# Huber loss, 8192 x 8192: another split of the element-wise work between VectorE and ScalarE, half-tile pieces, and a tail whose pieces are ordered by hand

## The chip, the cores and the metric

The kernel runs on one core of one Trainium2 chip. The metric is device time in microseconds for one execution of the whole kernel, the median of several executions. "Tile" below means one slab of 128 partitions by up to 10432 fp32 columns.

## The reference

```python
def reference(pred, target):            # both 8192 x 8192 fp32
    delta = 1.0
    diff = pred - target
    abs_diff = np.abs(diff)
    return np.where(abs_diff <= delta, 0.5 * diff**2, delta * (abs_diff - 0.5 * delta))
```

With d = pred - target the result is d*d/2 where |d| is at most 1, and |d| - 1/2 elsewhere. It is element-wise: every element of the two inputs is read once and every element of the result is written once, 268 MB each.

## The kernel before, in words

The three arrays are taken as flat, and cut into 51 tiles: 50 of 128 x 10432 elements (5216 KB each) and a last one, number 50, of 128 x 2688. A tile of prediction lives in one of three buffers `a` (`NA = 3`), a tile of target in one of two buffers `b` (`NB = 2`). The result is computed in place in `a` and stored from there.

*Transfers.* All loads and stores are issued by SyncE, in the order of the list `order` that `plan` builds. In the middle of the kernel one turn is: store tile i, load target of tile i+2, load prediction of tile i+3. SyncE takes them strictly in order: a transfer that must wait holds up all behind it. A store waits for the tile's last VectorE instruction; a target load waits until its buffer is free, that is until tile i has been computed; a prediction load waits until the store of tile i has landed, because it goes into the same buffer. In the page and the timeline the stores carry line L136 and the loads L145. For the last tiles `order` is written out one by one: `z` is the number of the last tile (50), and tiles 48 and 49 have their target loaded in two parts, columns 0 to 7040 (`h0`) and 7040 to 10432 (`h1`), so that the first part can be put ahead of other transfers.

*Compute.* Each tile is cut into three pieces of 3520, 3520 and 3392 columns (tile 50 into two of 1344). A piece goes through `first` and later through `second`:

- `first`: VectorE subtracts target from prediction into `a` (L97) and clamps the difference to [-1, 1] into `b` (L98). ScalarE then makes `a` absolute (L101), subtracts 1 and cuts off at 0 (Relu, L103), and squares `b` (L104).
- `second`: VectorE adds half of `b` to `a` (L113). This is the result, since min(|d|,1)^2 / 2 + max(|d|-1, 0) is the Huber loss. For the last piece of a tile (the set `vec`) VectorE also does the work of L103, as L110.

The list `comp` holds these steps in the order in which they are issued to the engines. VectorE and ScalarE each execute in that order. For most tiles it is first, first, second, first, second, second; for the last three tiles (`LAST`) the closing step of a tile is put behind the opening step of the next.

`compute_until` issues steps from `comp` until the tile, or the part of it, that the next transfer needs is finished. The engines' order is written out by hand in this way; the waits between engines are placed by the framework from what each instruction reads and writes, and from the release of buffers.

Of the kernel before, what the change touches and what calls it, by code (L numbers as in the profile page):

```python
# [1 line left out]

# [4 lines left out]

P = 128
W = 10432
NA, NB = 3, 2  # L10
LAST = 3


def plan(total):

    tiles = [(c, min(W, total - c)) for c in range(0, total, W)]
    n = len(tiles)
    wid = [w for _, w in tiles]

    def cut(i, k):
        step = -(-wid[i] // (k * 64)) * 64
        edge = list(range(0, wid[i], step)) + [wid[i]]
        return list(zip(edge, edge[1:]))

    whole = lambda kind, i: [(kind, i, 0, wid[i])]  # L30
    order = []
    for lo, hi in cut(0, 2):
        order += [("b", 0, lo, hi), ("a", 0, lo, hi)]
    order += whole("a", 1) + whole("b", 1) + whole("a", 2)

    z = n - 1
    for i in range(z - 6):
        order += whole("s", i) + whole("b", i + 2) + whole("a", i + 3)

    split = cut(z - 1, 3)[1][1]  # L40
    h0, h1 = (0, split), (split, W)
    order += whole("s", z - 6) + whole("b", z - 4) + whole("a", z - 3)
    order += whole("b", z - 3) + whole("s", z - 5)
    order += [("b", z - 2, *h0)] + whole("a", z - 2)
    order += whole("s", z - 4) + [("b", z - 2, *h1)]
    order += [("b", z - 1, *h0)] + whole("a", z - 1)
    order += whole("s", z - 3) + [("b", z - 1, *h1)]
    order += whole("b", z) + whole("a", z) + whole("s", z - 2)
    order += [("s", z - 1, lo, hi) for lo, hi in cut(z - 1, 3)]
    order += [("s", z, lo, hi) for lo, hi in cut(z, 2)]  # L50
    pieces = [(i, lo, hi) for i in range(n) for lo, hi in cut(i, 3 if wid[i] > W // 2 else 2)]
    comp = []
    late = []
    for p in pieces:
        comp.append(("first",) + p)
        late.append(p)
        i, lo, hi = p
        if i < n - LAST and hi == wid[i]:
            comp += [("second",) + q for q in late]
            late = []  # L60
        elif len(late) > 1:
            comp.append(("second",) + late.pop(0))
    comp += [("second",) + q for q in late]
    vec = {p for p in pieces if p[2] == wid[p[0]]}
    return tiles, order, comp, vec


@with_exitstack
def kernel(
    ctx: ExitStack,  # L70
    tc: tile.TileContext,
    pred: bass.AP,
    target: bass.AP,
    out: bass.AP,
):
    nc = tc.nc
    f32 = mybir.dt.float32
    Alu = mybir.AluOpType
    Act = mybir.ActivationFunctionType
    Eng = mybir.EngineType  # L80

    flat = {k: x.rearrange("r c -> (r c)") for k, x in zip("bas", (target, pred, out))}
    tiles, order, comp, vec = plan(flat["a"].shape[0] // P)

    const = ctx.enter_context(tc.tile_pool(name="const", bufs=1))
    pool_a = ctx.enter_context(tc.tile_pool(name="pool_a", bufs=NA))
    pool_b = ctx.enter_context(tc.tile_pool(name="pool_b", bufs=NB))

    neg1 = const.tile([P, 1], f32)
    nc.vector.memset(neg1, -1.0)  # L90

    A, B = {}, {}

    def first(i, lo, hi):

        a, b = A[i][:, lo:hi], B[i][:, lo:hi]
        nc.vector.tensor_tensor(out=a, in0=a, in1=b, op=Alu.subtract)  # L97
        nc.vector.tensor_scalar(  # L98
            out=b, in0=a, scalar1=-1.0, scalar2=1.0, op0=Alu.max, op1=Alu.min
        )  # L100
        nc.scalar.activation(out=a, in_=a, func=Act.Abs)  # L101
        if (i, lo, hi) not in vec:
            nc.scalar.activation(out=a, in_=a, func=Act.Relu, bias=neg1)  # L103
        nc.scalar.activation(out=b, in_=b, func=Act.Square)  # L104

    def second(i, lo, hi):

        a, b = A[i][:, lo:hi], B[i][:, lo:hi]
        if (i, lo, hi) in vec:
            nc.vector.tensor_scalar(  # L110
                out=a, in0=a, scalar1=-1.0, scalar2=0.0, op0=Alu.add, op1=Alu.max
            )
        nc.vector.scalar_tensor_tensor(  # L113
            out=a, in0=b, scalar=0.5, in1=a, op0=Alu.mult, op1=Alu.add
        )

    ready = {i: 0 for i in range(-max(NA, NB), len(tiles))}
    for i in range(-max(NA, NB), 0):
        ready[i] = W

    def compute_until(i, hi):
        while ready[i] < hi:
            what, j, l, h = comp.pop(0)
            if what == "first":
                first(j, l, h)
            else:
                second(j, l, h)
                ready[j] = h

    with tc.manual_schedule(engines={Eng.SP, Eng.DVE, Eng.Activation}):  # L130
        for kind, i, lo, hi in order:
            at, w = tiles[i]
            dram = flat[kind][P * at : P * (at + w)].rearrange("(p m) -> p m", p=P)
            if kind == "s":
                compute_until(i, hi)
                nc.sync.dma_start(out=dram[:, lo:hi], in_=A[i][:, lo:hi])  # L136
                continue
            have, pool, name, bufs = (
                (A, pool_a, "a", NA) if kind == "a" else (B, pool_b, "b", NB)
            )  # L140
            if i not in have:
                if i >= bufs:
                    compute_until(i - bufs, tiles[i - bufs][1])
                have[i] = pool.tile([P, W], f32, name=name)
            nc.sync.dma_start(out=have[i][:, lo:hi], in_=dram[:, lo:hi])  # L145


# [1 line left out]
_INS = ['pred', 'target']  # L149
_OUTS = [((8192, 8192), 'float32')]  # L150


# [23 lines left out]
```

## Time and profile before

| | |
|---|---|
| median of 9 runs | 1874.13 us (1874.03 to 1875.05) |
| the profiled execution's own time | 1875.05 us |
| span of that execution | 1873.3 us |
| VectorE busy | 1517.4 us, 81% |
| ScalarE busy | 1238.9 us, 66% |
| DMA | 805.41 MB, mean 430 GB/s |
| VectorE L97, 128 x 3520 | 3822 ns |
| VectorE L98, 128 x 3520 | 1994 ns |
| VectorE L113, 128 x 3520 | 3825 ns |
| ScalarE L101 / L103 / L104, 128 x 3520 | 3129 / 3229 / 3120 ns |
| SyncE waiting for stores to land, before a load | 1193.8 us in 48 waits |
| SyncE waiting for VectorE's L113, before a store | 467.9 us in 50 waits |

The span runs from the program's first instruction on any engine to its last; the own time of an execution is a little longer. In lines of the profile's timeline the first number is the start in microseconds from the span's start, the second the duration, then engine, source line, operation and what it writes and reads; a bracket at the end gives the idle time of the engine before the instruction and what ended it. `SPq` marks SyncE's issue of a transfer: the duration there is that of the issue, not of the transfer. DMA work is shown as a share of the 16 DMA engines' time and in GB/s.

### The profile page before, as it was taken

Reading aid. Unit: us, or ns where it says so; the run is one execution under the profiler, and the core shown is the slowest. Engines: PE = TensorE matmul, PEld = TensorE weight load, DVE = VectorE, ACT = ScalarE, POOL = GpSimd, SP = SyncE. Lnnn points to the kernel's source line nnn. Section 1 sums busy time; section 2 is a strip of 40 time slices with the busy share of each in tenths; the row PEclk is TensorE's granted clock in tenths of the full one; section 3 lists DMA queues with packets and bytes.
Section 4 is the critical chain, followed back from the end, with each engine's and each line's share of the span. In section 5 each row is a group of like instructions: output and inputs, shape, how many; then the busy total and the mean of one; then the engine's idle time right before and its main releaser. Section 6 shows DMA issues by size and latency. Waiting matters only on the chain.

```text
span 1873.3 us, 1374 instructions
## 1 busy us (share of the span) xinstructions
DVE 1517.4 (81%) x508; ACT 1238.9 (66%) x406; POOL 0.2 (0%) x4
## 2 busy tenths in 40 slices
DVE  5887878787788778887878787888778887878898
ACT  4567756765776577657756775676577657756776
POOL 0000000000000000000000000000000000000000
DMA  9999999999999999999999999999999999999999
GB/s 413 428 434 434 431 437 429 433 435 431 437 430 432 435 431 437 430 435 434 430 437 430 433 436 429 437 431 432 437 429 436 432 432 437 429 435 433 387 427 383
DMA packets 23051, 805.41 MB, mean 430 GB/s; under 512 B 2560, under 2 KB 2560, under 8 KB 2816
## 3 DMA queue, kind: packets, MB, share of 16 engines
q1 hardware_dynamic: 23040, 805.32, 99.8%
q14 instruction: 11, 0.09, 0.0%
HBM read 536.87 MB, written 268.44 MB: 430 GB/s over the span
## 4 chain that ended last, share of the span: by engine, by line
DMA 53%; DVE 25%; ACT 17%; issue 4%; SPq 1%; ACTq 0%; DVEq 0%
DMA b<-in_target_dram 46%; DVE a L97 10%; DVE a L113 10%; ACT b L104 8%; DVE b L98 5%; ACT a L101 4%; ACT a L103 4%; DMA out_dram<-a 4%; DMA a<-in_pred_dram 3%; SPq L136 0%; DVE a L110 0%; SPq L145 0%; ACTq L171 0%; DVEq L97 0%; DVEq L113 0%
## 5 line engine op out<-in xcount | busy, mean ns | idle before, releaser
L101 ACT ACTIVATE a<-a 128x3520 f32<-128x3520 f32 (+1 forms) x152 | 467.0, 3072 | 605.2 <-DVE b L98 598.4
L113 DVE SCALAR_TENSOR_TENSOR a<-b,a 128x3520 f32<-128x3520 f32 (+1 forms) x152 | 570.3, 3752 | 200.3 <-ACT b L104 200.1
L97 DVE TENSOR_TENSOR a<-a,b 128x3520 f32<-128x3520 f32 (+1 forms) x152 | 569.5, 3747 | 141.5 <-DMA b<-in_target_dram 119.4
L104 ACT ACTIVATE b<-b 128x3520 f32<-128x3520 f32 (+1 forms) x152 | 465.3, 3061 | 0.0
L103 ACT ACTIVATE a<-a,neg 128x3520 f32<-128x3520 f32 (+1 forms) x101 | 324.3, 3211 | 3.3
L98 DVE TENSOR_SCALAR b<-a 128x3520 f32<-128x3520 f32 (+1 forms) x152 | 297.4, 1957 | 5.2
L110 DVE TENSOR_SCALAR a<-a 128x3392 f32<-128x3392 f32 (+1 forms) x51 | 96.9, 1899 | 0.0
L101 ACT ACT_TABLE_LOAD x1 | 1.3, 1283 | 16.3 <-DMA a<-in_pred_dram 16.3
L90 DVE MEMSET neg<- 128x1 f32 x1 | 0.1, 59 | 0.8 <-PEq L160 0.8
L160 POOL MEMSET const-bfloat16-1.0<- 128x1 bf16 x1 | 0.1, 103 | 0.0
L160 POOL MEMSET const-uint8-127<- 128x1 uint8 x1 | 0.1, 103 | 0.0
L160 POOL MEMSET const-float32-1.0<- 128x1 f32 x1 | 0.1, 100 | 0.0
L160 POOL MEMSET const-float32-0.0<- 128x1 f32 x1 | 0.1, 99 | 0.2 <-issue 0.2
## 6 DMA issues: line engine op xcount, KB each, us to landing
a<-in_pred_dram SPq DMA_DIRECT2D x49, 5216.0 KB, 24.6
out_dram<-a SPq DMA_DIRECT2D x49, 5216.0 KB, 27.1
b<-in_target_dram SPq DMA_DIRECT2D x47, 5216.0 KB, 39.0
b<-in_target_dram SPq DMA_DIRECT2D x2, 3520.0 KB, 13.6
out_dram<-a SPq DMA_DIRECT2D x2, 1760.0 KB, 17.2
b<-in_target_dram SPq DMA_DIRECT2D x2, 1696.0 KB, 39.1
b<-in_target_dram SPq DMA_DIRECT2D x1, 2624.0 KB, 8.9
a<-in_pred_dram SPq DMA_DIRECT2D x1, 2624.0 KB, 15.1
```

What stands on the lines that cost most here:

```text
L90: nc.vector.memset(neg1, -1.0)
L97: nc.vector.tensor_tensor(out=a, in0=a, in1=b, op=Alu.subtract)
L98: nc.vector.tensor_scalar(out=b, in0=a, scalar1=-1.0, scalar2=1.0, op0=Alu.max, op1=Alu.min)
L101: nc.scalar.activation(out=a, in_=a, func=Act.Abs)
L103: nc.scalar.activation(out=a, in_=a, func=Act.Relu, bias=neg1)
L104: nc.scalar.activation(out=b, in_=b, func=Act.Square)
L110: nc.vector.tensor_scalar(out=a, in0=a, scalar1=-1.0, scalar2=0.0, op0=Alu.add, op1=Alu.max)
L113: nc.vector.scalar_tensor_tensor(out=a, in0=b, scalar=0.5, in1=a, op0=Alu.mult, op1=Alu.add)
L160: nc = _bacc.Bacc("TRN2", target_bir_lowering=False, num_devices=1)
```

## The change

Tiles 0 to 45 are computed in two pieces, of 5248 and 5184 columns, by three steps, each done for both pieces before the next:

- `d`: VectorE subtracts; ScalarE makes the difference absolute, in `a`.
- `t`: VectorE forms t = min(|d|, 1) * |d| in place; ScalarE copies t/2 into `b`.
- `h`: VectorE takes max(t - 1/2, t/2), the result. (For |d| at most 1, t = d*d and t/2 is the larger; beyond it, t = |d| and t - 1/2 is the larger.)

The last five tiles keep the former method (`f` and `g`; with capital letters VectorE does L103's work in place of ScalarE). Their order is written out piece by piece in `TAIL`: the letter is the step, the first number counts tiles back from the last, the second is the piece. `F4.0` is the opening step of piece 0 of tile 46, `g3.2` the closing step of piece 2 of tile 47.

Tiles 46 to 49 have their target loaded in two parts (before: 48 and 49), and the order of the transfers near the end is changed: the second part of tile 48's target stands ahead of the store of tile 46, and tile 49's first target part behind that store, as before. `compute_until` now goes by columns that are closed, since pieces of a tile no longer close in order.

```diff
-LAST = 3
+TAIL = """
+F4.0 f4.1 G4.0 f4.2 g4.1 f3.2 F3.1 g4.2 F3.0 G3.1 G3.0 F2.0 F2.1 f2.2 G2.1 g3.2 G2.0 g2.2
+F1.0 f1.1 G1.0 f1.2 f0.0 g1.1 f0.1 g1.2 g0.0 g0.1
+"""
...
-    split = cut(z - 1, 3)[1][1]
-    h0, h1 = (0, split), (split, W)
-    order += whole("s", z - 6) + whole("b", z - 4) + whole("a", z - 3)
-    order += whole("b", z - 3) + whole("s", z - 5)
-    order += [("b", z - 2, *h0)] + whole("a", z - 2)
-    order += whole("s", z - 4) + [("b", z - 2, *h1)]
-    order += [("b", z - 1, *h0)] + whole("a", z - 1)
+    third = cut(z - 1, 3)
+    h0, h1 = (0, third[1][1]), third[2]
+    order += whole("s", z - 6) + [("b", z - 4, *h0), ("b", z - 4, *h1)]
+    order += whole("a", z - 3) + [("b", z - 3, *h0), ("b", z - 3, *h1)]
+    order += whole("s", z - 5)
+    order += [("b", z - 2, *h0)] + whole("a", z - 2) + [("b", z - 2, *h1)]
+    order += whole("s", z - 4) + [("b", z - 1, *h0)] + whole("a", z - 1)
     order += whole("s", z - 3) + [("b", z - 1, *h1)]
     order += whole("b", z) + whole("a", z) + whole("s", z - 2)
-    order += [("s", z - 1, lo, hi) for lo, hi in cut(z - 1, 3)]
+    order += [("s", z - 1, lo, hi) for lo, hi in third]
     order += [("s", z, lo, hi) for lo, hi in cut(z, 2)]
...
+    comp = [(op, i, lo, hi) for i in range(z - 4) for op in "dth" for lo, hi in cut(i, 2)]
+    for word in TAIL.split():
+        back, piece = word[1:].split(".")
+        i = z - int(back)
+        comp.append((word[0], i, *cut(i, 3 if i < z else 2)[int(piece)]))
+    return tiles, order, comp
...
+        if op == "d":
+            sub(a, b)
+            act(out=a, in_=a, func=Act.Abs)
+        elif op == "t":
+            vec.scalar_tensor_tensor(
+                out=a, in0=a, scalar=1.0, in1=a, op0=Alu.min, op1=Alu.mult
+            )
+            act(out=b, in_=a, func=Act.Copy, scale=0.5)
+        elif op == "h":
+            vec.scalar_tensor_tensor(
+                out=a, in0=a, scalar=-0.5, in1=b, op0=Alu.add, op1=Alu.max
+            )
+        elif op in "fF":
+            sub(a, b)
+            vec.tensor_scalar(
+                out=b, in0=a, scalar1=-1.0, scalar2=1.0, op0=Alu.max, op1=Alu.min
+            )
+            act(out=a, in_=a, func=Act.Abs)
+            if op == "f":
+                act(out=a, in_=a, func=Act.Relu, bias=neg1)
+            act(out=b, in_=b, func=Act.Square)
+        else:
+            if op == "G":
+                vec.tensor_scalar(
+                    out=a, in0=a, scalar1=-1.0, scalar2=0.0, op0=Alu.add, op1=Alu.max
+                )
+            vec.scalar_tensor_tensor(
+                out=a, in0=b, scalar=0.5, in1=a, op0=Alu.mult, op1=Alu.add
+            )
+        if op in "hgG":
+            left[i] -= hi - lo
+            closed.update((i, c) for c in range(lo, hi, 64))
...
-                compute_until(i, hi)
+                compute_until(lambda: all((i, c) in closed for c in range(lo, hi, 64)))
...
-                    compute_until(i - bufs, tiles[i - bufs][1])
+                    compute_until(lambda: left[i - bufs] == 0)
```

## The prediction

> **What bounds the kernel now.** I read the page's totals first, then its slices.
>
> ```profile
> span 1873.3 us, 1374 instructions
> DVE 1517.4 (81%) x508; ACT 1238.9 (66%) x406; POOL 0.2 (0%) x4
> ...
> DMA  9999999999999999999999999999999999999999
> GB/s 413 428 434 434 431 437 429 433 435 431 437 430 432 435 431 437 430 435 434 430 437 430 433 436 429 437 431 432 437 429 436 432 432 437 429 435 433 387 427 383
> ```
>
> VectorE is at 81%, but the DMA engines are busy in every slice at about 433 GB/s. A full tile transfer (128 x 10432 fp32, 5.34 MB) therefore takes 5.34/0.433 = 12.34 us, and a tile's three transfers 37.0 us. Only the first slice and the last three are short. Next the timeline of a middle tile, DMA issues and VectorE's first operation:
>
> ```profile
> 942.00 0.34 SPq L136 DMA_DIRECT2D out_dram<-a  x1
> 942.43 0.38 SPq L145 DMA_DIRECT2D b<-in_target_dram  x1
> 944.56 3.83 DVE L97 TENSOR_TENSOR a<-a,b 128x3520 f32<-128x3520 f32 x1 [2.59 <-DMA b<-in_target_dram]
> ...
> 969.12 0.33 SPq L145 DMA_DIRECT2D a<-in_pred_dram  x1
> ...
> 979.03 0.34 SPq L136 DMA_DIRECT2D out_dram<-a  x1
> ```
>
> The period is 979.03 - 942.00 = 37.03 us: DMA's 37.0. VectorE waits 2.59 us per tile for target. The store issued at 979.03 queues behind a prediction load that runs to about 969.1 + 24.6 (the page's median to landing) = 993.7, so compute has some 14.7 us of slack there. Last the end of the kernel, as windows (start:end, length, busy of DVE, ACT and POOL, clock, DMA share, GB/s) and timeline:
>
> ```profile
> 1750.00:1752.00 2.00, 2.00 (x2) 2.00 (x2) 0.00 (x0) 1.00 1.01 438
> 1752.00:1754.00 2.00, 1.57 (x2) 1.45 (x1) 0.00 (x0) 1.00 0.68 292
> 1754.00:1756.00 2.00, 2.00 (x1) 0.00 (x0) 0.00 (x0) 1.00 0.24 104
> 1756.00:1758.00 2.00, 2.00 (x2) 0.00 (x0) 0.00 (x0) 1.00 0.12 46
> 1758.00:1760.00 2.00, 2.00 (x1) 0.00 (x0) 0.00 (x0) 1.00 0.99 296
> ```
> ```profile
> 1753.49 3.69 DVE L113 SCALAR_TENSOR_TENSOR a<-b,a 128x3392 f32<-128x3392 f32 x1 [0.43 <-ACT b L104]
> ...
> 1757.21 0.33 SPq L145 DMA_DIRECT2D b<-in_target_dram  x1
> 1760.43 0.33 SPq L145 DMA_DIRECT2D a<-in_pred_dram  x1
> ```
>
> The queue runs dry once: about 0.3 + 0.76 + 0.88 of each 2 us, some 3.8 us of an average engine. The load that ends it, tile 48's first target part, goes out at 1757.21, just after tile 46's *last* VectorE operation ends (1753.49 + 3.69 = 1757.18), though it overwrites only columns 0 to 7040, which were finished at 1751.2. A target buffer is released as a whole tile. And at least one DMA engine was not dry: 0.12 of 16 engines is two still storing tile 45, whose landing let the 1760.43 issue go. That last engine lags the rest by some 5 us (they stop about 1754, it about 1760), loses nothing in the gap, and sets the end.
>
> **The Trainium skill.** "DMA: Bandwidth & Descriptors", section "Anatomy of one DMA — SWDGE (gpsimd) path", says that DMA engines do not wait on semaphores; the issuing sequencer does, and they eat their queues. The trace agrees: each late SP issue shows as missing GB/s. Its section "Why a DMA increments its semaphore by 16 and not by 1" says that the engines finish independently and only the full count means landed: the drain from share 0.68 to 0.12 shows that skew. "VectorE: DVE Perf Modes", section "The TRN2 errata — SBUF-src ops pay a fixed extra latency per instruction", gives (N+151)/0.96 ns for fp32 tensor_tensor; at 3520 that is 3824 ns, the trace has 3822, and SCALAR_TENSOR_TENSOR 3825.
>
> **The change, part by part.**
> *Steady tiles 0 to 45.* Per tile it removes three subtracts, three clamps, three combines and one Relu on VectorE (33 us busy) and adds two each of subtract, the new t and the new max step, on 5248 and 5184 columns. No row has those widths; from the subtract's groups by shape, 1344 (1552) and 3520 (3822), the slope is 1.043 ns, so 5.62 and 5.56 us. t reads one tile on both inputs, which no row does; at best 2.9 us (twice as fast, like a clamp), at worst 11 us (each element fetched twice); I take 5.62, as for L113's two inputs. Back-to-back operations overlap 0.08 us, so a tile is 3 x (5.62 + 5.56) - 0.4 = 33.1 us. ScalarE's half-tile Abs or Copy, scaled from 3129 and 3029 ns, takes about 4.6 us, less than the VectorE half behind which it hides. 33.1 is below 37.03, and below today's first-operation-to-store 34.5, so stores go out about 1 us earlier into a backlog of 14.7: worth 0. Without the DMA cover it would be 46 x 37 again only if t passed 7.5 us.
> *First tile.* Compute starts when its second half lands (28.6), and ends near 56.3 against 53.5; the loads queued run to about 65: 0.
> *Split target loads.* Tiles 46 and 47 give two more DMA instructions, 0.4 us of SP each behind a backlog: 0, 0.8 uncovered.
> *The hand-ordered tail* is what counts. In the built program the load of tile 48's first target part still waits for VectorE's last piece of tile 46 (g4.2), and tile 49's for the last piece of tile 47 (g3.2). Both were moved later.
>
> First gap. g4.2 now stands behind f3.2 and F3.1, which need tile 47's second target part. Target 46 landed just before 1722.74; prediction 47 and target 47 follow, 2 x 12.34, so 1747.4. Then subtract 3.68, clamp 1.93, subtract 3.82, clamp 1.99, g4.2 3.69, with overlaps 15.1: the load issues at 1762.5 instead of 1757.2 and flows 1 us later (as 1757.21 did near 1758.2), at 1763.5. The lagging engine ends tile 45's store about 1760.1, so it now stands 3.4 us; before, 0. The others stand some 9.
>
> Second gap. Behind it SP issues at once prediction 48, the rest of target 48 and store 46: 3 tiles, 37.0 us, dry at 1800.5 on all engines. g3.2 stands behind tile 48's F2.0, F2.1, f2.2 and G2.1. Prediction 48 lands after 8.3 + 12.3 us, plus 0.3, at 1784.5; VectorE has finished all else by about 1780 and waits. Then 3.82 + 1.99, the same again, 3.68 + 1.93, 1.99 + 3.83, 3.69: 26.7 us, and the load of tile 49 issues at 1811.2, flows at 1812.2. In the SP queue prediction 49, store 47, the rest of target 49 and tile 50 stand behind that wait, so nothing else can flow. Gap 11.7 us.
>
> From 1812.2 five full transfers and three of 2688 columns remain, 61.7 + 9.5 = 71.2 us. The final stores are issued under backlog: VectorE needs about 41 us for tiles 49 and 50 after prediction 49 lands near 1833, against 1883.
>
> Sum: 3.4 + 11.7 = +15.1 us. Given back: before, 108.3 us of data after the lagging engine's 1760.1 should have ended at 1868.4 and ended about 1872 (small last transfers, engine skew); over the last 71.2 us the same drag is 2/3, so -1.2. The shorter instruction streams may drag the lagging engine less, 0 to -2; I take -0.9. Net +13.0: span 1886.3 on the profile's own basis (its execution took 1875.05, 1.75 over its span; the median shown, 1874.13, is 0.83 over), so 1887 for the median, +0.7%.
>
> **Rivals.**
> *Release by columns (not slower).* If tile 48's and 49's first target parts went as soon as columns 0 to 7040 are done, they would issue near 1745 and 1780, before 1760 and 1800; both gaps vanish. At most the 3.8 us of today's gap is won, at least nothing because the lagging engine never stood: 1870.3 to 1874. For it: the order of the tail only makes sense so. Against: 1757.21, and the waits of the built program. It decides if the second load issues before 1800.5.
> *Only the first gap.* If g3.2 came before tile 48's pieces reach VectorE, +3.4 - 2.1: 1875.4, no difference. Against: VectorE runs in order and g3.2 is written behind them.
> *VectorE becomes the bound.* If t took 8 us in place of 5.6, a tile would be 33.1 + 4.8 = 37.9 and 46 tiles lose 0.9 each, 41 us, on top of the gaps: 1928. For it: only 3.9 us of slack per tile. Against: same form and width as L113. It decides at 7.5 us.
>
> **How the numbers follow.** Two gaps: 0.86. Release by columns 0.04, three quarters of it faster. Only the first gap or a smaller lag that hides most: 0.06, no difference. VectorE bound: 0.04, slower. So faster 0.03, same 0.07, slower 0.90 (about 0.2%, 3.7 us, is what a measurement of this kernel can tell). The range is the forecast's own: low end with no lag of the slow engine into the tail (-5) and a little less drag, 1881; high end with none of the give-back and two more microseconds of skew, 1891.
>
> **What would show it.** Right: tile 48's first target load issued near 1762.5 and tile 49's near 1811; windows with almost no GB/s from about 1801 to 1812; VectorE idle near 1780 to 1784.5, waiting for DMA; mid-kernel period still 37.0, with VectorE waits for target of about 3.9 us a tile; VectorE busy near 1676 us (46 x 33.5 + 134), ScalarE near 935. Wrong: GB/s unbroken to the end (columns), or a mid-kernel period above 37.2 (VectorE). A lag of the slowest engine that differs from 5 us would move the first gap and the end together.

## The result, and the profile after

The changed kernel takes 1889.26 us (median of 9 runs, 1887.99 to 1890.04) against 1874.91 us for the kernel before beside it (29 runs): ratio 1.0076, 95% interval 1.0067 to 1.0084. It is 0.76% slower. The forecast was 1887, range 1881 to 1891. The profiled execution has a span of 1888.3 us and took 1890.04.

The page of the changed kernel, totals and slices:

```profile
span 1888.3 us, 1008 instructions
DVE 1655.2 (88%) x325; ACT 937.6 (50%) x221; POOL 0.2 (0%) x4
...
DMA  9999999999999999999999999999999999999879
GB/s 410 436 427 437 430 432 436 428 435 434 430 436 430 433 437 430 433 438 429 435 433 430 438 430 433 436 430 434 437 429 436 434 430 435 432 431 436 337 317 407
```

VectorE gained 138 us of work and ScalarE lost 301 us, and up to slice 37 GB/s does not show it. The loss is all in slices 38 and 39, 337 and 317 where 433 was usual. In two slices of 47.2 us that is (96 + 116)/433 x 47.2 = 23.1 us of missing transfers; the same two slices before, 387 and 427, missed (46 + 6)/433 x 46.8 = 5.6 us. The last slice is fuller than before, 407 against 383, which is 2.6 us the other way. Together that is 14.9 us, the difference of the spans.

The timeline of a middle tile, SyncE's issues and VectorE (xN at the end: so many instructions merged into the line):

```profile
903.73 0.34 SPq L148 DMA_DIRECT2D out_dram<-a  x1
904.17 0.38 SPq L157 DMA_DIRECT2D b<-in_target_dram  x1
...
932.14 0.33 SPq L157 DMA_DIRECT2D a<-in_pred_dram  x1
940.66 0.34 SPq L148 DMA_DIRECT2D out_dram<-a  x1
941.10 0.38 SPq L157 DMA_DIRECT2D b<-in_target_dram  x1
944.56 11.09 DVE L95 TENSOR_TENSOR a<-a,b 128x5248 f32<-128x5248 f32 x2 [3.92 <-DMA b<-in_target_dram]
```

The period is 940.66 - 903.73 = 36.93 us, as before, and VectorE waits 3.92 us for target where it waited 2.59. It still starts its tile at 944.56, as in the kernel before: DMA sets the pace.

Now the two places that were named in the forecast: SyncE's issues near the end, and VectorE around the second of them.

```profile
1718.22 0.81 SPq L157 DMA_DIRECT2D b<-in_target_dram  x2
1719.07 0.43 SPq L148 DMA_DIRECT2D out_dram<-a  x1
1761.94 0.33 SPq L157 DMA_DIRECT2D b<-in_target_dram  x1
1762.31 0.43 SPq L157 DMA_DIRECT2D a<-in_pred_dram  x1
1762.79 0.43 SPq L157 DMA_DIRECT2D b<-in_target_dram  x1
1763.26 0.56 SPq L148 DMA_DIRECT2D out_dram<-a  x1
1812.16 0.33 SPq L157 DMA_DIRECT2D b<-in_target_dram  x1
```
```profile
1758.23 3.68 DVE L131 SCALAR_TENSOR_TENSOR a<-b,a 128x3392 f32<-128x3392 f32 x1
...
1785.47 3.83 DVE L95 TENSOR_TENSOR a<-a,b 128x3520 f32<-128x3520 f32 x1 [6.13 <-DMA a<-in_pred_dram]
...
1804.66 7.43 DVE L131 SCALAR_TENSOR_TENSOR a<-b,a 128x3520 f32<-128x3520 f32 x2
```

Tile 48's first target part goes out at 1761.94, when g4.2 ends (1758.23 + 3.68 = 1761.91). Tile 49's goes out at 1812.16; the two merged operations at 1804.66 are the closing steps of tile 48's piece 1 and of tile 47's piece 2, g3.2, and end at 1812.09. From 1761.94 on SyncE sends four transfers at once, the first part of tile 48's target among them, and then nothing for 48 us. The windows (busy of DVE, ACT, POOL, clock, DMA share, GB/s) show the DMA engines empty each time:

```profile
1756.00:1758.00 2.00, 1.97 (x2) 2.00 (x1) 0.00 (x0) 1.00 0.10 42
1758.00:1760.00 2.00, 2.00 (x2) 2.00 (x2) 0.00 (x0) 1.00 0.00 0
1760.00:1762.00 2.00, 2.00 (x2) 2.00 (x2) 0.00 (x0) 1.00 0.00 0
...
1800.00:1802.00 2.00, 1.97 (x2) 2.00 (x2) 0.00 (x0) 1.00 0.77 334
1802.00:1804.00 2.00, 2.00 (x2) 2.00 (x2) 0.00 (x0) 1.00 0.00 0
...
1810.00:1812.00 2.00, 2.00 (x1) 2.00 (x1) 0.00 (x0) 1.00 0.00 0
```

### The profile page after: what moved, and what is told of

Its sections match the earlier page's. It is cut to its first block, busy times and chain, and to the rows that moved or that the text cites. A ratio compares the mean times of both kernels' runs of the same rounds, so it can differ in the third digit from the quotient of the medians.

```text
span 1888.3 us, 1008 instructions
## 1 busy us (share of the span) xinstructions
DVE 1655.2 (88%) x325; ACT 937.6 (50%) x221; POOL 0.2 (0%) x4
## 4 chain that ended last, share of the span: by engine, by line
DMA 61%; DVE 36%; issue 1%; ACT 1%; SPq 1%; ACTq 0%; DVEq 0%
DMA b<-in_target_dram 57%; DVE a L95 12%; DVE a L109 11%; DVE a L114 10%; DMA a<-in_pred_dram 4%; DVE a L131 1%; DVE b L119 1%; SPq L148 0%; ACT a L122 0%; ACT b L125 0%; DVE a L128 0%; ACT a L124 0%; SPq L157 0%; ACTq L183 0%; DVEq L95 0%
## 5 line engine op out<-in xcount | busy, mean ns | idle before, releaser
L107 ACT ACTIVATE a<-a 128x5248 f32<-128x5248 f32 x92 | 418.6, 4550 | 785.0 <-DVE a L95 785.0
L95 DVE TENSOR_TENSOR a<-a,b 128x5248 f32<-128x5248 f32 (+3 forms) x106 | 558.8, 5307 | 218.0 <-DMA b<-in_target_dram 131.1
L109 DVE SCALAR_TENSOR_TENSOR a<-a 128x5248 f32<-128x5248 f32 x92 | 510.0, 5585 | 0.0
L114 DVE SCALAR_TENSOR_TENSOR a<-a,b 128x5248 f32<-128x5248 f32 x92 | 510.0, 5585 | 0.0
L112 ACT ACTIVATE b<-a 128x5248 f32<-128x5248 f32 x92 | 418.6, 4550 | 87.6 <-DVE a L109 87.6
L122 ACT ACTIVATE a<-a 128x3520 f32<-128x3520 f32 (+2 forms) x14 | 39.7, 2839 | 65.5 <-DVE b L119 65.5
L131 DVE SCALAR_TENSOR_TENSOR a<-b,a 128x3520 f32<-128x3520 f32 (+2 forms) x14 | 48.3, 3461 | 3.8 <-ACT b L125 3.2
L125 ACT ACTIVATE b<-b 128x3520 f32<-128x3520 f32 (+2 forms) x14 | 39.6, 2830 | 0.0
L119 DVE TENSOR_SCALAR b<-a 128x3520 f32<-128x3520 f32 (+2 forms) x14 | 25.4, 1813 | 0.5
L124 ACT ACTIVATE a<-a,neg 128x3392 f32<-128x3392 f32 (+2 forms) x8 | 21.8, 2722 | 0.3
## 6 DMA issues: line engine op xcount, KB each, us to landing
a<-in_pred_dram SPq DMA_DIRECT2D x1, 2624.0 KB, 14.9
```

The lines of the kernel that those rows point to most:

```text
L107: act(out=a, in_=a, func=Act.Abs)
L109: vec.scalar_tensor_tensor(out=a, in0=a, scalar=1.0, in1=a, op0=Alu.min, op1=Alu.mult)
L112: act(out=b, in_=a, func=Act.Copy, scale=0.5)
L114: vec.scalar_tensor_tensor(out=a, in0=a, scalar=-0.5, in1=b, op0=Alu.add, op1=Alu.max)
L119: vec.tensor_scalar(out=b, in0=a, scalar1=-1.0, scalar2=1.0, op0=Alu.max, op1=Alu.min)
L122: act(out=a, in_=a, func=Act.Abs)
```

## The experiments

A *gap* is a stretch in which the DMA engines have nothing to transfer. The theory (A): both gaps come from the whole-tile release of the target buffers together with the place of g4.2 and g3.2 in VectorE's order. The rivals: the steady method itself costs (B); the split loads and the new order of transfers cost (C); and, for what sets the end, the latest of the 16 DMA engines against the average one.

**Both closing steps early.** An edit of the changed kernel:

```diff
-F4.0 f4.1 G4.0 f4.2 g4.1 f3.2 F3.1 g4.2 F3.0 G3.1 G3.0 F2.0 F2.1 f2.2 G2.1 g3.2 G2.0 g2.2
+F4.0 f4.1 G4.0 f4.2 g4.1 g4.2 f3.2 F3.1 F3.0 G3.1 G3.0 g3.2 F2.0 F2.1 f2.2 G2.1 G2.0 g2.2
```

> The changed kernel with only two words of its tail moved: the closing steps of the last piece of tile 46 (g4.2) and of tile 47 (g3.2) stand directly behind the other closing steps of their tile. Theory A (a target buffer is released only by the tile's last VectorE piece, and those two pieces were written too late): tile 48's first target load issues near 1754 instead of 1761.9, tile 49's near 1788 instead of 1812.2, both before the DMA queue is dry on its last engine (about 1759 and 1800), so both gaps close for that engine and about 15 us come back: 1873 to 1875 us. Rival B (the steady half-tile method, with VectorE at 88%, is what costs): nothing comes back, 1888 to 1890. Rival C (the split target loads and the new order of the transfers cost by themselves): something between, 1878 to 1885.

1871.25 us, ratio to the kernel before 0.998 (0.9972 to 0.9987). The issues of the two target parts in the timeline of this kernel:

```profile
1753.19 0.33 SPq L157 DMA_DIRECT2D b<-in_target_dram  x1
...
1787.50 0.33 SPq L157 DMA_DIRECT2D b<-in_target_dram  x1
```

Two words moved in the tail give back 18 us, more than the 14 that the change had lost and 2 us more than the best that was expected. B and C fall as causes of the loss, since both are still in this kernel.

**Only g3.2 early.**

```diff
-F4.0 f4.1 G4.0 f4.2 g4.1 f3.2 F3.1 g4.2 F3.0 G3.1 G3.0 F2.0 F2.1 f2.2 G2.1 g3.2 G2.0 g2.2
+F4.0 f4.1 G4.0 f4.2 g4.1 f3.2 F3.1 g4.2 F3.0 G3.1 G3.0 g3.2 F2.0 F2.1 f2.2 G2.1 G2.0 g2.2
```

> The changed kernel with only g3.2 moved up, behind the other closing steps of tile 47. Theory A: the second gap (about 11.5 us) closes, the first stays at about 4 us on the last engine: tile 49's first target load issues near 1784, about 1877 to 1879 us. If the two gaps did not add, or the second was only the echo of the first, the time would stay near 1885 or fall to 1874. Rival B: 1889.

1876.58 us, ratio 1.0006 (1.0 to 1.0013), a little under what was expected. The second gap alone is worth 1889.3 - 1876.6 = 12.7 us; tile 49's first target load issues at 1782.61. The first gap stays (tile 48's load issues at 1761.54), and leaves this kernel 5.3 us over the one above.

**Only g4.2 early.**

```diff
-F4.0 f4.1 G4.0 f4.2 g4.1 f3.2 F3.1 g4.2 F3.0 G3.1 G3.0 F2.0 F2.1 f2.2 G2.1 g3.2 G2.0 g2.2
+F4.0 f4.1 G4.0 f4.2 g4.1 g4.2 f3.2 F3.1 F3.0 G3.1 G3.0 F2.0 F2.1 f2.2 G2.1 g3.2 G2.0 g2.2
```

> The changed kernel with only g4.2 moved up, behind the other closing steps of tile 46. Theory A: tile 48's first target load issues near 1754 and the first gap closes for the last engine, but g3.2 still hangs on prediction 48, which cannot flow before the queue in front of it is done: tile 49's first target load stays near 1811, so the second gap only starts earlier and takes over most of what the first gave back: 1886 to 1889 us, hardly faster. If the gaps were independent, 4 us would come back: 1885.

1889.12 us, ratio 1.0075 (1.0061 to 1.0088): nothing came back. The windows of this kernel show why:

```profile
1752.00:1756.00 4.00, 4.00 (x2) 0.00 (x0) 0.00 (x0) 1.00 0.89 328
1756.00:1760.00 4.00, 3.96 (x3) 1.05 (x1) 0.00 (x0) 1.00 0.97 419
1790.00:1794.00 4.00, 3.97 (x2) 4.00 (x2) 0.00 (x0) 1.00 0.72 313
1794.00:1798.00 4.00, 4.00 (x2) 4.00 (x2) 0.00 (x0) 1.00 0.07 31
1798.00:1802.00 4.00, 3.97 (x3) 4.00 (x3) 0.00 (x0) 1.00 0.00 0
```

The first gap is filled but for about 1 us of an average engine, so the four transfers behind it end sooner: the last of them lands at 1797.19, in the changed kernel at 1803.07. But g3.2 still waits for VectorE's work on tile 48, and the next load goes out at 1810.62, hardly sooner than 1812.16. What the first gap gave back, the second took: it now begins earlier. The two gaps therefore do not add as independent costs: repairing the first is worth about 5 us only when the second is repaired.

**Release by columns, the order of pieces as it is.** The two target buffers are allocated once, so that the framework sees one buffer written again, and waits column by column:

```diff
-                have[i] = pool.tile([P, W], f32, name=name)
+                if kind == "b" and i >= bufs:
+                    have[i] = have[i - bufs]
+                else:
+                    have[i] = pool.tile([P, W], f32, name=name)
```

> The changed kernel, its tail as it is, but the two target buffers are allocated once and used again, so that a load into columns 0 to 7040 waits only for the pieces that cover them. Theory A with whole-tile release as its cause: tile 48's first target load issues near 1745 and tile 49's near 1780, no gap is left on any engine, 1873 to 1875 us (the engine that ends last never stood in the kernel before, so nothing more than that is won there), at best 1870. If it was only the order of the pieces, whatever the release, the time stays at 1889.

1869.19 us, ratio 0.9971 (0.9959 to 0.9982). The first target parts of tiles 48 and 49 issue at these times, long before g4.2 and g3.2 have run; in the changed kernel it was 1761.94 and 1812.16:

```profile
1743.90 0.33 SPq L160 DMA_DIRECT2D b<-in_target_dram  x1
...
1778.30 0.33 SPq L160 DMA_DIRECT2D b<-in_target_dram  x1
```

With whole-tile release taken away, the hand-ordered tail is harmless; the order alone was not the cause, nor the release alone. Of all kernels run, this one and its variant with whole loads (below) are the fastest, 0.29% under the kernel before, and faster than the 1870 us that was expected at best. The page, DMA row by row of slices:

```profile
DMA  9999999999999999999999999999999999999999
GB/s 415 429 429 436 434 430 432 434 434 431 433 437 429 434 437 429 434 435 433 431 434 436 430 434 435 431 434 434 433 431 435 434 430 434 435 431 433 432 433 387
```

**The same release in the kernel before.** The same edit, applied to the kernel before.

> The kernel before with the two target buffers allocated once and used again, so that the load of tile 48's first target part waits for the pieces over columns 0 to 7040 alone and issues near 1751 instead of 1757.2. The 3.8 us of missing DMA work at 1752 to 1758 should go. Theory (the end is set by the one DMA engine that never stood in that gap): the other engines win 3.8 us, the last engine nothing, 1873.5 to 1875 us. Rival (the gap is paid by the kernel): 1870 to 1871 us.

1873.78 us, ratio 0.9994 (0.9986 to 1.0002): no difference that can be told, though the gap is gone. Windows of this kernel, to be set beside 292, 104, 46 and 296 GB/s of the kernel before:

```profile
1752.00:1754.00 2.00, 1.62 (x1) 2.00 (x1) 0.00 (x0) 1.00 1.02 418
1754.00:1756.00 2.00, 1.95 (x1) 0.02 (x1) 0.00 (x0) 1.00 0.93 393
1756.00:1758.00 2.00, 2.00 (x2) 0.00 (x0) 0.00 (x0) 1.00 0.86 373
1758.00:1760.00 2.00, 2.00 (x1) 0.00 (x0) 0.00 (x0) 1.00 1.05 447
```

An average engine no longer stands for those 3.8 us, and the 1870 to 1871 us of the rival did not come: the late engine sets the end, as the forecast had it. A smaller gain cannot be ruled out. In the profiled execution (table below) the last engine reached the store of tile 45 0.8 us later than in the kernel before, and then lost 1.8 us less to the end.

**The steady method alone.** The kernel before, its tail and its transfers untouched, with tiles 0 to 45 computed by steps d, t and h:

```diff
-    pieces = [(i, lo, hi) for i in range(n) for lo, hi in cut(i, 3 if wid[i] > W // 2 else 2)]
-    comp = []
+    comp = [(op, i, lo, hi) for i in range(z - 4) for op in "dth" for lo, hi in cut(i, 2)]
+    pieces = [(i, lo, hi) for i in range(z - 4, n) for lo, hi in cut(i, 3 if wid[i] > W // 2 else 2)]
... (a function `steady` with the three steps of the changed kernel, and its call in `compute_until`)
```

> The kernel before with tiles 0 to 45 computed by the new method (two pieces, steps d, t, h), and its own tail and its own order of transfers. Theory A: the steady method hides under DMA entirely (33.1 us of VectorE per 37.0 us): 1873.5 to 1875 us. Rival B (VectorE at 88% costs): 1880 or more, up to the 1889 of the whole change.

1872.64 us, ratio 0.9987 (0.998 to 0.9993). Not only hidden: 0.13% faster, with VectorE at 88%. The forecast had put the steady part at 0, and in a separate term a gain of up to 2 us for shorter instruction streams. The 0.13% is of the size of that term, but its cause is not shown (last section).

**VectorE's slack, one clamp more per tile.** The changed kernel with one more operation, which changes no value, in step `t` ahead of its first instruction:

```diff
+            if lo == 0:
+                vec.tensor_scalar(
+                    out=a, in0=a, scalar1=-1e30, scalar2=1e30, op0=Alu.max, op1=Alu.min
+                )
```

> The changed kernel with one more VectorE operation per steady tile, a clamp to plus or minus 1e30 (which changes no value) ahead of step t on the first half tile, about 2.9 us. VectorE then needs about 36.0 us per tile against DMA's 37.0. Theory: hidden, 1889 to 1890 us. Rival (VectorE is already at the edge): 46 x up to 2.9, up to 2020 us.

1890.23 us, ratio 1.0081 (1.0066 to 1.0097), against 1.0076 without the clamp: hidden.

**Two clamps more per tile.** The same without the condition, so that both halves of a tile have the clamp.

> As the run before, with the clamp on both halves: about 5.7 us more, 38.8 us of VectorE per tile against DMA's 37.0. Theory: VectorE is now the bound and each of the 46 tiles costs about 1.8 to 1.9 us more, the tail's gaps stay: 1889 + 85 = about 1970 to 1980 us. If it stays below 1900, VectorE's slack is larger than 3.9 us.

1978.43 us, ratio 1.0552 (1.0532 to 1.0571). The timeline of a middle tile; there is no wait left ahead of the subtract:

```profile
915.90 11.09 DVE L95 TENSOR_TENSOR a<-a,b 128x5248 f32<-128x5248 f32 x2
...
926.91 2.88 DVE L110 TENSOR_SCALAR a<-a 128x5248 f32<-128x5248 f32 x1
...
935.37 2.85 DVE L110 TENSOR_SCALAR a<-a 128x5184 f32<-128x5184 f32 x1
```

Two clamps of 2.88 and 2.85 us cost 89 us, 1.94 per tile: 5.73 - 1.94 = 3.8 us was VectorE's slack, close to the 3.92 us that it waited for target. The rival that VectorE becomes the bound was a real edge, 3.8 us away.

**More instructions.** The kernel with release by columns, with ten one-column fills more per steady tile, five in each step h:

```diff
... (`spare` is a tile of one column that nothing reads)
+            for _ in range(5):
+                vec.memset(spare, 0.0)
```

> The changed kernel with target buffers released by columns, plus ten one-column fills per steady tile on VectorE (460 instructions in all, into a spare column that nothing reads). VectorE has 3.9 us of slack per tile and a fill takes about 0.06 us, so compute is not touched. Theory D (part of the last DMA engine's lag comes from the fetch of instructions, 8 KB each, of which the kernel before has 11 in its span and the changed one 8): about 4 more fetches, each holding one engine for up to 0.8 us, 0 to 3 us more than the 1869.2 without the fills, and the fetches are seen in the trace. If the lag has another cause, 1869 to 1870 us.

1878.8 us, ratio 1.0019 (1.0012 to 1.0026), 9.6 us more than without the fills: three times the most that was expected. The page has 12 transfers on the instruction queue, taken here for fetches of instructions (8192 bytes each in the trace), against 8 of that size without the fills:

```profile
q14 instruction: 12, 0.10, 0.0%
```

The trace has 16 landing records per transfer, one for each DMA engine that has finished its share; they do not name the engine, but the last of the 16 says how late the latest engine is. In the middle of this kernel that engine loses 0.96 to 0.98 us five times, on the transfers under way at 385, 682, 979, 1247 and 1543 us, and these are the times of five of the fetches. At those of 367, 566, 1158 and 1504 us it loses nothing, so it is not every fetch that falls on it. By the store of tile 45 it is 8.53 us behind (table in the next section), against 4.42 without the fills. The rest, more than half of the 9.6 us, is lost after that, in the tail. The loads there wait for stores that the late engine has yet to finish: prediction 48 issues at 1762.31, just after the store of tile 45 has landed at 1762.29. On that load eleven of the 16 landings fall 1.3 to 1.5 us further back and the three just ahead of the last less than 0.1: the engines in front had run dry while the late ones still had work. The other losses in this tail were not taken apart.

**Whole target loads for tiles 46 and 47.** The kernel with release by columns, and:

```diff
-    order += whole("s", z - 6) + [("b", z - 4, *h0), ("b", z - 4, *h1)]
-    order += whole("a", z - 3) + [("b", z - 3, *h0), ("b", z - 3, *h1)]
+    order += whole("s", z - 6) + whole("b", z - 4)
+    order += whole("a", z - 3) + whole("b", z - 3)
```

> The changed kernel with target buffers released by columns, and the targets of tiles 46 and 47 loaded whole again instead of in two parts. The parts are then worth nothing for the release, since tile 46's and 47's buffers were free long before. Expected: no difference from the run with the parts, 1869 to 1870.5 us; if the smaller transfers cost DMA time by themselves, up to 0.2 us less.

1869.37 us, ratio 0.9973 (0.9964 to 0.9982): no difference. With release by columns the split loads are worth nothing and cost nothing, as in the forecast; with whole-tile release this was not tried.

## Why the prediction was right, and what in it was off

A full transfer takes 12.33 us between landings in mid-kernel. If all transfers followed each other at that pace, the last would land near 1862 us. What the last engine is behind that pace is called its delay here, and what it loses in the tail outside the gaps is the drag. From the landing records, in us, one profiled execution each:

| kernel | delay at store 45 | delay at the end | of it in the tail |
|---|---|---|---|
| before | 6.51 | 10.41 | 3.9 |
| changed | 5.47 | 25.53 | 20.1 |
| both early | 4.69 | 6.13 | 1.4 |
| only g3.2 early | 5.15 | 12.05 | 6.9 |
| only g4.2 early | 4.90 | 24.26 | 19.4 |
| release by columns | 4.42 | 4.67 | 0.2 |
| the same in the kernel before | 7.28 | 9.39 | 2.1 |
| steady method alone | 6.13 | 9.28 | 3.2 |
| more instructions | 8.53 | 14.15 | 5.6 |

Release by columns beats the kernel before by 2.1 us of delay at store 45 and by 3.7 us in the tail.

*Steady tiles, 0.* Right. 5625 and 5552 ns were measured for the two widths against 5.62 and 5.56, and step t, which reads one tile twice, took 5619 ns: the middle of its three values. VectorE's total was put at 1676 us and is 1655, because the durations were added without the 0.08 us by which neighbours overlap. The 33 us of VectorE work that the forecast takes away per tile is a wrong sum (its own durations give 30.5), but nothing rests on it.

*The first tile and the split loads, 0.* Right; the first store went out at 56.04 (forecast 56.3), with the DMA queue full.

*First gap, load at 1762.5.* Right at 1761.94. For the last engine it was put at 3.4 us; the landing of tile 48's first part came 5.48 us late. That engine was 0.9 us less late than assumed when its work ended (1759.20 for 1760.1), and part of the rest is a restart: the first packet of each of the 16 engines after the gap, a row of 28160 bytes, took 1.28 to 1.82 us where 1.04 is usual.

*Second gap, load at 1811.2, 11.7 us.* Right at 1812.16, and 11.71 us on the last engine.

*The give-back, -1.2 and -0.9.* Half right, and the mis-sized part of the sum. The engine's delay at store 45 did fall, by 6.51 - 5.47 = 1.04 us in these two executions; it is 4.4 to 6.1 in the six kernels of the table that have the new steady method without the fills, and 6.5 and 7.3 in the two that have the old one. The drag fell by 1.0, from 3.9 to 20.1 - 5.5 - 11.7 = 2.9. That this is near the forecast's 1.2 is luck: it was scaled with the data left to transfer, as the cost of small last transfers and of skew, and the records show it on a few loads. In the kernel before, 3.5 of the 3.9 us stand on predictions 48, 49 and 50 (1.28, 0.59 and 1.66); in the changed kernel, 2.6 of the 2.9 on two loads after the gaps (1.41 and 1.20; the echo below). But a delay that falls ahead of the first gap cannot be deducted beside it: the gap ends when VectorE is done, so an engine that is less late only stands longer. The -0.9 was counted once too often, with the restart on top. So 15.1 us between the last landings (25.53 - 10.41) stand against a sum of 13.0, and the span is 1888.3 in place of 1886.3.

*"DMA engines do not wait on semaphores"*, from the Trainium skill, "DMA: Bandwidth & Descriptors", "Anatomy of one DMA — SWDGE (gpsimd) path", carried the argument. The run with only g4.2 early agrees: four transfers that SyncE sent 4 to 9 us sooner end 6 us sooner on the last engine, and the engines then stand at 0 GB/s until SyncE's next issue at 1810.62.

*The rivals.* Release by columns was the right reading of what the tail's order needs, and becomes true with four lines. "Only the first gap" was priced at 1875.4 and measured, as its own kernel, at 1876.6. VectorE as the bound was put at 7.5 us for step t, and the two-clamp run puts the slack at 3.8 us per tile, which two steps t would use up at 5.6 + 1.9 = 7.5 us each.

## What to carry to other kernels

In a kernel at the DMA limit, price an edit by the latest moment at which each load may be issued without the queue running dry, and follow what that issue waits for back into the compute engines' orders: here one closing step of 3.7 us, g3.2, written behind work on the next tile, held up five transfers. Ask what a buffer's release is tied to, its last reader or the reader of those columns. And when two stalls stand behind each other, test them one by one and together: the first gap was worth 0.1 us alone and 5.3 us after the second was gone.

## What the runs showed that was not expected

*Late engines and the instruction fetches.* The engines do not lag alike: on the store of tile 44 in the kernel before, eleven of the 16 landings lie within 0.7 us, and the other five follow 1.5 to 5.2 us after these. In the kernel with more instructions, each of the five steps of 0.96 to 0.98 us of the latest engine falls on a transfer under way at a fetch, though a fetch of 8 KB itself lasts 0.31 to 0.33 us, and 460 fills of some 0.06 us on an engine with 3.8 us to spare per tile made the kernel 9.6 us slower. In the kernel before, the last engine lost 0.69, 0.97 and 0.79 us on the transfers under way at its fetches of 980.6, 1386.8 and 1757.6. That fewer instructions are why the steady method alone gains 0.13% fits these numbers, but in its profiled execution, one of its slower ones (1873.77 us), only 0.4 us stands in the delay at store 45, so it is not shown. The larger part of the engine's lag at store 45 is of another kind: in every kernel of the table 4.2 to 4.8 us of it are there by the store of tile 16, built up mostly on prediction loads (0.47, 0.61 and 1.02 us on those of tiles 3, 4 and 5 in the kernel before). Its cause is open.

*An echo after a gap.* Some 17 to 26 us after engines had stood, a short stretch follows in which nearly all packets are slow; it is called an echo here. The windows of the changed kernel, after the gap that ended at 1813:

```profile
1830.00:1832.00 2.00, 0.00 (x0) 0.00 (x0) 0.00 (x0) 1.00 1.39 522
1832.00:1834.00 2.00, 0.00 (x0) 0.00 (x0) 0.00 (x0) 1.00 1.26 334
1834.00:1836.00 2.00, 0.00 (x0) 0.00 (x0) 0.00 (x0) 1.00 0.44 188
```

The mean of the six microseconds is 348 GB/s, which is 6 x (433 - 348)/433 = 1.2 us of transfers lost; all 16 packets of 41728 bytes that start in the microsecond from 1833 take 2.5 us on average where 1.54 is usual, and the last engine's landing slips by 1.20 us. There is one such stretch after each gap of the changed kernel (1.41 and 1.20 us), one after the gap of the kernel before (1.28 us on prediction 48), and one in the run with both steps early (1.17), where only part of the engines had stood. With release by columns, where none stood, the last engine loses 0.2 us in the whole tail. A gap seems to cost about a microsecond more than its length; why the engines stumble a transfer later was not tried, and stays open.
